# Reciprocal roots through Ln and Exp, and a final norm in three token parts, in a hybrid SSD and attention step on one core

## The chip, the cores and the metric

The kernel runs on one core of a Trainium2 chip. A core has five engines with a queue each: TensorE (PE in the profile, with its weight loads as PEld), VectorE (DVE), ScalarE (ACT), GpSimd (POOL, unused here) and SyncE (SP), which issues most DMA transfers. Each engine works through its own instructions in order and waits on semaphores for the others. The metric is the device time of one execution in microseconds (us).

## What is computed

One inference step of two layers over 640 tokens (512 latent, 128 prompt) and 1024 features: a Mamba-2 style SSD mixer in layer 0, differential attention in layer 1, a convolutional feed-forward block after each, and a final norm. Each sub-layer starts from a root mean square norm, and this norm is what the change rewrites:

```
def _rms(x):
    xf = x.astype(F32)
    return xf * lax.rsqrt(jnp.mean(xf * xf, axis=-1, keepdims=True) + EPS)

def rmsnorm(x, g):
    return (_rms(x) * g.astype(F32)).astype(x.dtype)

def modulate(x, g, shift, scale):
    return rmsnorm(x, g) * (1 + scale) + shift

def conv_ffn(h, up_w, conv_w, conv_b, down_w):
    u = dwconv(h @ up_w, conv_w, conv_b)
    a, v = jnp.split(u, 2, axis=-1)
    return (jax.nn.silu(a) * v) @ down_w

for i in range(DEPTH):
    x = x + gate_mix * mixer[i % 2](modulate(x, norm_mix_g, shift, scale))
    x = x + gate_ffn * conv_ffn(modulate(x, norm_ffn_g, shift, scale))
y = rmsnorm(x, final_norm_g)
```

The loop is a shortened form of the reference's own. In the SSD mixer the output is also normed in four feature groups, and in attention each of the eight heads' outputs is normed over its 128 features; all of these take a reciprocal root per token.

## The kernel before

**Layout.** Activations are feature-major: `x` is eight tiles of 128 features by 640 tokens. Tokens fall in two "halves", A = columns 0 to 255 and B = columns 256 to 639, the last 128 of which are the prompt. Every dense product is done in three passes, with weights and activations each split in a rounded high part and the rest (`whi`, `wlo` and `h..h`, `h..l`): high by high, high by low, low by high. A weight tile arrives by DMA in `raw`, ScalarE copies it to `whi` (line 131) and VectorE subtracts to get `wlo` (line 132).

**Order of the work.** The class `Step` emits dense products as the main stream. Other work is written as generators in a queue of tasks: after each feature tile of a product a hook (line 71) advances every task that is due, and a generator's `yield n` says in how many hooks it wants to go on. A scheduler of the language then orders each engine's instructions, so that an engine's own order can differ from the order of the code; the groups of VectorE operations in a root are interleaved with other work in the trace.

**PSUM.** Dense products and attention scores share a pool of three two-bank tiles (tag `d`). Sums `ms`, transposes and broadcasts use one bank with tag `m` or one with tag `y`.

**The root.** `rms_bcast` (line 173) sums squares over features with a matrix of ones on TensorE (`ms`, four groups of a quarter of the tokens), calls `rsqrt` (line 161), yields, and then spreads the result to all partitions with a selecting matrix (`nbc` for the norms of `x`, `obc` for a head, `gbc` for an SSD group). `rsqrt` works on 128 by n values, n a quarter of the tokens: 64 for A, 96 for B, 160 for all tokens. It is a scale and shift (`rs_v`, line 166), an integer seed (line 167) and three Newton steps of three VectorE operations each (lines 169 to 171), eleven in all. It is called 21 times: once at the start, four times in the SSD mixer (`ssd_norm`), for both halves of the three norms between sub-layers (`norm_task`), for the eight heads (`att_tail`) and for both halves of the final norm (`final_task`).

**The end of a sub-layer.** `project_last` (line 259) makes the eight output tiles. The first five are done one after the other for both halves. The last three are done half by half: first A for each of the three tiles, then B, tile 5 alone and tiles 6 and 7 together. After a tile's product `gate_add` (line 247) adds it to `x` on VectorE and `norm_sq` squares it on ScalarE. Behind a half's last tile the next norm for this half is queued with a delay of three hooks.

**The final norm.** `final_task` (line 1001) forms, per half, eight output tiles `yt` on VectorE, in temporary buffers that rotate over four, each followed by its DMA issue on SyncE. At the end of the program the queued tasks are run to their ends in order (line 1069).

**Attention.** Per head, `att_head` makes a score product `sl` into a `d` tile for each of four query blocks and two maps, VectorE takes row maxima (`sm`), ScalarE the exponentials `e` with their sums, and `att_tail` transposes the weights (`wt`), multiplies them with the values (`ov`), takes the squares (`osq`) and the head's root. This runs between the products of the next head's q, k and v tiles.

**Activation tables.** [...] The kernel before uses Tanh, Exp, Silu, Square, Copy and Identity.

## Time and profile before

| What | us |
|---|---|
| Runs of the kernel, median of 3 (lowest, highest) | 1979.58 (1979.57, 1981.41) |
| Profiled execution, first to last instruction (span) | 1977.5 |
| TensorE busy in it | 1905.5 |
| VectorE busy | 1418.0 |
| ScalarE busy | 905.2 |

The profiled execution's own device time is not recorded beside its span; the median of the runs lies 2.1 us above the span. In the views below, a row of the timeline has the start, the duration, the engine, the line, the operation and what it writes and reads; in square brackets stands the idle time of the engine before it and what ended that. A row of the windows has the window and its length, then the busy time and number of instructions of PE, PEld, DVE, ACT and POOL, then the granted TensorE clock as a share of full speed, the DMA share and GB/s. A row of the groups has the count, the busy time and the mean of one in ns, then the idle time ahead.

### The profile page before, as it was taken

What the parts mean: (1) busy time and instruction counts of PE and PEld (TensorE: products, weight loads), DVE (VectorE), ACT (ScalarE), POOL (GpSimd) and SP (SyncE); (2) the same over time, 40 slices, a digit from 0 to 9 for tenths busy, and PEclk for the clock granted to TensorE, in tenths of its full rate; (3) what the DMA queues carried; (4) which work ended last, traced back from release to release, by engine and by line L of the source; (5) the groups of instructions that cost most, each with busy time, mean ns of one, the idle gap of its engine ahead of it and who ended that gap; (6) DMA issues with size and microseconds to landing.
All of it is one profiled execution on the core that took longest, in us unless ns stands there. A gap on an engine that the chain in (4) does not pass through costs nothing.

```text
span 1977.5 us, 33157 instructions
## 1 busy us (share of the span) xinstructions
PE 1905.5 (96%) x13453; PEld 1788.0 (90%) x13453; DVE 1418.0 (72%) x2745; ACT 905.2 (46%) x1702; POOL 0.2 (0%) x4
## 2 busy tenths in 40 slices
PE   6899999999999999999999989999999999999997
PEld 3678989888999999999999978988899999999997
DVE  4658899998977888688675788888868553553554
ACT  2337677676834432133133466666635331331331
POOL 0000000000000000000000000000000000000000
PEclk9999999999999999999999989999999999999999
DMA  8454212112232244444442221111022222222211
GB/s 303 153 191 143 75 44 81 49 65 79 91 98 68 96 149 141 144 142 142 144 136 70 70 69 38 49 49 38 21 93 75 75 75 75 77 67 83 73 57 54
DMA packets 62121, 184.98 MB, mean 94 GB/s; under 512 B 7824, under 2 KB 14224, under 8 KB 61840
## 3 DMA queue, kind: packets, MB, share of 16 engines
q1 hardware_dynamic: 61968, 182.86, 28.4%
q8 instruction: 106, 1.74, 0.4%
q14 instruction: 47, 0.39, 0.1%
HBM read 177.06 MB, written 5.77 MB: 92 GB/s over the span
## 4 chain that ended last, share of the span: by engine, by line
PE 76%; DMA 11%; DVE 7%; ACT 3%; issue 3%; SPq 0%; DVEq 0%; ACTq 0%
PE up L99 19%; PE po L99 18%; DMA mw<-in_modT 10%; PE z L99 6%; PE x L99 5%; PE st L99 5%; DVE junk L454 3%; PE bc L99 3%; PE yp L99 3%; PE q L99 3%; PE k L99 2%; PE v L99 2%; PE sl L99 2%; PE modrow L99 1%; PE ov L99 1%
## 5 line engine op out<-in xcount | busy, mean ns | idle before, releaser
L90 ACT ACTIVATE whi<-raw 128x1024 fp32r<-128x1024 f32 (+4 forms) x230 | 235.9, 1027 | 422.4 <-PE po L99 182.3
L96 DVE TENSOR_TENSOR wlo<-raw,whi 128x1024 fp32r<-128x1024 f32 (+4 forms) x230 | 270.2, 1177 | 164.2 <-ACT whi L90 162.8
L93 DVE SCALAR_TENSOR_TENSOR xr<-po,mod,xr 128x256 f32<-128x256 f32 (+1 forms) x231 | 89.7, 434 | 125.6 <-PE po L99 125.4
L454 DVE CUSTOM_DVE_ANT_0 junk<-mw,cbc 128x1024 f32<-128x1024 f32 x96 | 116.4, 1221 | 75.7 <-DMA mw<-in_modT 75.6
L99 PE MATMUL po<-mh,whi 128*128 128x256 f32 (+1 forms) x704 | 167.8, 310 | 0.8 <-DVE ca L93 0.8
L99 PE MATMUL po<-mh,wlo 128*128 128x256 f32 (+1 forms) x704 | 167.3, 310 | 0.0
L99 PE MATMUL po<-ml,whi 128*128 128x256 f32 (+1 forms) x704 | 167.2, 309 | 0.0
L99 PE MATMUL up<-h01h,whi 128*128 128x256 f32 (+1 forms) x656 | 151.3, 312 | 9.7 <-DVE ca L93 5.8
L99 PE MATMUL up<-h11h,whi 128*128 128x256 f32 (+1 forms) x656 | 149.4, 309 | 2.7 <-DVE ca L93 2.7
L99 PE MATMUL up<-h01l,whi 128*128 128x256 f32 (+1 forms) x656 | 150.4, 310 | 0.0
L99 PE MATMUL up<-h01h,wlo 128*128 128x256 f32 (+1 forms) x656 | 150.4, 310 | 0.0
L99 PE MATMUL up<-h11h,wlo 128*128 128x256 f32 (+1 forms) x656 | 149.4, 309 | 0.0
L99 PE MATMUL up<-h11l,whi 128*128 128x256 f32 (+1 forms) x656 | 149.4, 309 | 0.0
L99 PEld LDWEIGHTS up<-h01h,whi 128*128 128x128 f32 x656 | 119.8, 189 | 11.9 <-issue 8.1
L99 PEld LDWEIGHTS po<-mh,whi 128*128 128x128 f32 x704 | 128.3, 188 | 1.3 <-issue 1.0
L99 PEld LDWEIGHTS po<-mh,wlo 128*128 128x128 f32 x704 | 128.4, 188 | 0.0
L99 PEld LDWEIGHTS po<-ml,whi 128*128 128x128 f32 x704 | 128.2, 188 | 0.2 <-DVE ml L96 0.2
L99 PEld LDWEIGHTS up<-h11h,whi 128*128 128x128 f32 x656 | 119.3, 188 | 3.0 <-ACT whi L90 3.0
L99 PEld LDWEIGHTS up<-h01l,whi 128*128 128x128 f32 x656 | 120.4, 189 | 0.0
L99 PEld LDWEIGHTS up<-h01h,wlo 128*128 128x128 f32 x656 | 120.3, 189 | 0.0
L99 PEld LDWEIGHTS up<-h11h,wlo 128*128 128x128 f32 x656 | 119.3, 188 | 0.0
L99 PEld LDWEIGHTS up<-h11l,whi 128*128 128x128 f32 x656 | 119.3, 188 | 0.0
(489 smaller groups left out, 4451.3 us busy)
## 6 DMA issues: line engine op xcount, KB each, us to landing
raw<-in_w_up SPq DMA_DIRECT2D x88, 512.0 KB, 3.5
mw<-in_modT SPq DMA_DIRECT2D x48, 512.0 KB, 4.4
raw<-in_w_in SPq DMA_DIRECT2D x40, 512.0 KB, 3.6
mr<-in_mod SPq DMA_DIRECT2D x32, 512.0 KB, 4.0
raw<-in_w_dn SPq DMA_DIRECT2D x32, 448.0 KB, 3.3
raw<-in_w_qkv SPq DMA_DIRECT2D x24, 512.0 KB, 3.5
mp<-in_modp SPq DMA_DIRECT2D x32, 256.0 KB, 5.4
raw<-in_w_so SPq DMA_DIRECT2D x16, 512.0 KB, 3.6
```

Of the source, the lines that this page charges most:

```text
L90: return self.nc.scalar.activation(out, in_, func, **k)
L93: return self.nc.vector.scalar_tensor_tensor(out, in0, s, in1, op0, op1)
L96: return self.nc.vector.tensor_tensor(out, a, b, op)
L99: return self.nc.tensor.matmul(out, lhsT, rhs, start=start, stop=stop)
L454: nc.vector.tensor_tensor_reduce(j, w, cb[:, c, :], 1.0, 0.0, ALU.mult, ALU.add, self.mod[l][:, t, c:c + 1])
```

## The change

Every root but those of the SSD groups takes its first value from two ScalarE functions, exp(-0.5 ln(ms / count + eps)), and then makes one Newton step instead of three. The last `project_last` of the program (in the feed-forward block of layer 1) makes its last three tiles in three token parts, A (256 columns), M (256, the rest of the latent tokens) and Q (128, the prompt). Its last group differs too: M and Q do the three tiles one by one, and only a part named B does tiles 6 and 7 together. The final norm has these three parts. A and M write each output tile to a buffer of the large pool and issue its DMA on SyncE; M waits 99 hooks after its broadcast, which leaves its outputs to the end; Q writes all eight outputs into one tile and issues two DMAs of four tiles each, the first on SyncE and the second on ScalarE. The remaining tasks are run to their ends last first. Comments and docstrings go, which is all that most of the diff does; those parts are left out here.

```diff
-HALF = {"A": (A0, A1), "B": (A1, B1)}
+HALF = {"A": (A0, A1), "B": (A1, B1), "M": (A1, TS), "Q": (TS, B1)}
-COND = {"A": ((0, 256, 1),), "B": ((256, 512, 1), (512, 640, 0))}
+COND = {"A": ((0, 256, 1),), "B": ((256, 512, 1), (512, 640, 0)), "M": ((256, 512, 1),), "Q": ((512, 640, 0),)}
...
-    def rsqrt(self, y, ms, n, count):
+    def rsqrt(self, y, ms, n, count, power):
         V.tensor_scalar(v, ms, 1.0 / count, EPS, ALU.mult, ALU.add)
-        V.tensor_scalar(y.bitcast(I32), v.bitcast(I32), -0.5, RSQRT_MAGIC, ALU.mult, ALU.add)
-        for _ in range(3):
+        if power:
+            self.act(y, ms, AF.Ln, scale=1.0 / count, bias=self.eps)
+            self.act(y, y, AF.Exp, scale=-0.5)
+        else:
+            V.tensor_scalar(y.bitcast(I32), v.bitcast(I32), -0.5, RSQRT_MAGIC, ALU.mult, ALU.add)
+        for _ in range(1 if power else 3):
...
-    def rms_bcast(self, alloc, sq, t0, t1, count, wait=4):
+    def rms_bcast(self, alloc, sq, t0, t1, count, wait=4, power=True):
-        self.rsqrt(y, ms[:, :n], n, count)
+        self.rsqrt(y, ms[:, :n], n, count, power)
...
-        tag = {"A": "y", "B": "m"}[half]
+        tag = {"A": "y", "B": "m", "M": "y", "Q": "m"}[half]
...
-    def project_last(self, h, ks, g, nextnorm, ks_last=None):
+    def project_last(self, h, ks, g, nextnorm, ks_last=None, parts="AB"):
...
-        for hf, groups in (("A", (ws[0:1], ws[1:2], ws[2:3])), ("B", (ws[0:1], ws[1:3]))):
-            for grp in groups:
+        for hf in parts:
+            for grp in ((ws[0:1], ws[1:3]) if hf == "B" else (ws[0:1], ws[1:2], ws[2:3])):
...
+        self.eps = self.ct([P, 1], "eps")
+        nc.vector.memset(self.eps, EPS)
...
-                self.project_last(mid, range(k0, k1), self.gate(l, 1), nextnorm)
+                self.project_last(mid, range(k0, k1), self.gate(l, 1), nextnorm, parts="AMQ" if l else "AB")
...
-        bc = yield from self.rms_bcast(lambda: self.wide("gbc"), [sq], 0, T, 512)
+        bc = yield from self.rms_bcast(lambda: self.wide("gbc"), [sq], 0, T, 512, power=False)
...
-    def final_task(self, half):
-        bc = yield from self.norm_stats(half)
-        c0, c1 = HALF[half]
+    def final_task(self, part):
+        nc = self.nc
+        bc = yield from self.norm_stats(part)
+        c0, c1 = HALF[part]
+        if part == "M":
+            yield 99
+        gain = lambda i: self.gains[:, 4 * KT + i:4 * KT + i + 1]
+        if part == "Q":
+            n = c1 - c0
+            y = self.pw.tile([P, 1024], F32, tag="raw", name="yq", bufs=RAW)
+            for i in range(KT):
+                self.stt(y[:, i * n:(i + 1) * n], self.x[i][:, c0:c1], gain(i), bc[:, :n], ALU.mult, ALU.mult)
+                if i % 4 == 3:
+                    eng = nc.sync if i == 3 else nc.scalar
+                    eng.dma_start(self.a["yT"][i - 3:i + 1, :, c0:c1].rearrange("i p c -> p i c"),
+                                  y[:, (i - 3) * n:(i + 1) * n].rearrange("p (i c) -> p i c", i=4))
+            return
         for i in range(KT):
-            t = self.tmp("yt")
-            self.stt(t[:, c0:c1], self.x[i][:, c0:c1], self.gains[:, 4 * KT + i:4 * KT + i + 1], bc[:, :c1 - c0],
-                     ALU.mult, ALU.mult)
-            self.nc.sync.dma_start(self.a["yT"][i, :, c0:c1], t[:, c0:c1])
+            t = self.slot("f", f"yt{i}", bufs=NF)
+            self.stt(t[:, c0:c1], self.x[i][:, c0:c1], gain(i), bc[:, :c1 - c0], ALU.mult, ALU.mult)
+            nc.sync.dma_start(self.a["yT"][i, :, c0:c1], t[:, c0:c1])
             yield 1
...
-            for t in list(self.tasks):
+            for t in reversed(list(self.tasks)):
                 self.drain(t)
```

## The prediction

> **What bounds the kernel now.** I read the page's totals first, then busy time by stage, then the chain of waits at the end.

> ```profile
> span 1977.5 us, 33157 instructions
> PE 1905.5 (96%) x13453; PEld 1788.0 (90%) x13453; DVE 1418.0 (72%) x2745; ACT 905.2 (46%) x1702; POOL 0.2 (0%) x4
> L90 ACT ACT_TABLE_LOAD x4 | 5.1, 1283 | 2.9 <-DVE sg L816 1.7 <-PEq L1160 0.7 <-DVE ca L93 0.5
> 1120.00:1480.00 360.00, 342.30 (x2237) 315.38 (x2237) 292.14 (x606) 225.65 (x455) 0.00 (x0) 0.98 0.15 49
> ```

> TensorE (PE, the first pair in a window's row) is busy 96% of the span, so an edit counts only where it starts or stops TensorE waiting, or shortens the end, where TensorE has run dry. The third row counts ScalarE's activation-table loads: four in the whole program, 1.28 us each. In attention (1120 to 1480) TensorE is idle only 18 us of 360, ScalarE (the fourth pair) is busy 226.

> **The change part by part.**

> *Table loads.* Of the 21 reciprocal roots, the four group norms of the SSD mixer keep the old form. The other 17 and one more (the final norm now has three parts) become 18 with Ln and Exp. In the changed program's ScalarE order every one of these 18 has a table load ahead of its Ln and another ahead of its Exp: 39 loads where there were 4 (with the first one, and two ahead of Silu; the old load ahead of the attention's first Exp is gone). ScalarE therefore gets 35 x 1.28 = 45 us of loads.

> [...]

> *DVE's relief.* A root loses the integer seed and two of three Newton steps, seven VectorE operations, and gains two ScalarE ones.

> ```profile
> 1964.51 0.27 DVE rs_v L166
> 1967.39 0.27 DVE rs_y L93
> 1967.80 2.01 PE nbc L99 x8
> L90 ACT ACTIVATE m<-r,Ctok 128x128 f32<-128x128 f32 x160 | 61.9, 387 | 0.0
> ```

> Uncontended, the old chain (eleven VectorE operations, the first and the last shown) runs from 1964.51 to 1967.66: 3.15 us, 0.29 each. The new one is the scale (0.27), Ln, a load (1.28), Exp and three VectorE operations (0.85). Ln and Exp are not in the trace; the nearest row, a ScalarE op with a bias operand on 128x128, has 0.39, and I take 0.3 (between 0.2, the smallest ops here, and 0.4). Sum 3.0 us when ScalarE idles long enough to hide the load ahead of Ln, up to 4.3 when not. The chain gains nothing, and ScalarE is blocked for 2 x 1.28 + 0.3 = 2.9 us up to the end of the second load. Seven VectorE operations saved per root lie in stages where TensorE does not wait for them: worth 0 to 0.5 us each time, I take 0.

> *Attention, eight roots.* Heads 1 to 5 repeat every 37.3 us; of head 4's norm:

> ```profile
> 1335.09 0.80 ACT L90 ACTIVATE e<-sl,sm 128x640 f32<-128x640 f32 x1
> 1335.86 0.80 ACT L90 ACTIVATE e<-sl,sm 128x640 f32<-128x640 f32 x1
> 1336.56 0.20 ACT L90 ACTIVATION_READ_ACCUMULATOR e<-sl,sm 128x1 f32 x1
> 1336.04 0.56 PE L99 MATMUL q<-h10h,whi 128*128 128x256 f32 x2 [1.07 <-ACT e L90]
> 1337.02 0.46 PE L99 MATMUL sl<-kh,qs 128*128 128x320 f32 x2
> ```

> The softmax exponentials `e` free the three rotating PSUM tiles; TensorE already waits 1.07 us for the first. The order listing puts load, Ln, load exactly between these two exponentials. The second then ends at 1336.76 + 2.9 = 1339.7, and the score product of 1337.02, which takes its PSUM tile, stands at the head of TensorE's queue until then, with the rest of the q tile behind it: 2.65 us each, 13.3 for five.

> ```profile
> 1199.23 0.28 ACT L90 ACTIVATE wpT<-wpt 128x128 f32<-128x128 f32 x1 [0.40 <-PE wpt L934]
> 1199.92 0.60 PE L951 MATMUL wt<-cst,w 128*128 128x128 f32 x4
> 1411.25 0.80 ACT L90 ACTIVATE e<-sl,sm 128x640 f32<-128x640 f32 x1 [0.84 <-DVE sm L890]
> 1412.33 0.46 PE L99 MATMUL sl<-kh,qs 128*128 128x320 f32 x2
> ```

> Head 0's loads stand ahead of the weight cast and the copy `wpT` that frees the bank for the transposes of 1199.92: the copy ends near 1203.5, 3.6 us of wait. Head 6 has 0.84 us of ScalarE idle to absorb: 2.35 late at 1411.25, 2.2 at 1412.33. Head 7's root falls in an idle ScalarE: 0. Together 19.1 us; lower bound 10 (half hidden by rescheduled gaps), upper 24 (no gap absorbs).

> *Clock.* Such waits also cost TensorE its clock:

> ```profile
> 654.20 0.87 PE L99 MATMUL up<-h01h,whi 128*128 128x256 f32 x2 [3.52 <-ACT whi L90]
> 654.20:657.00 2.80, 2.80 (x10) 2.80 (x11) 2.74 (x7) 1.99 (x2) 0.00 (x0) 0.50 0.00 0
> 840.51 0.53 PE L99 MATMUL up<-h01h,whi 128*128 128x256 f32 x2 [2.28 <-DVE ca L93]
> 841.50:845.00 3.50, 3.50 (x15) 3.50 (x15) 2.25 (x3) 2.36 (x3) 0.00 (x0) 0.54 0.40 138
> 1515.46 0.54 PE L99 MATMUL up<-h11h,whi 128*128 128x256 f32 x2 [2.75 <-DVE ca L93]
> 1515.50:1518.50 3.00, 3.00 (x21) 3.00 (x22) 2.94 (x8) 2.10 (x3) 0.00 (x0) 1.00 0.02 5
> ```

> The granted clock (third figure from the end) is 0.50 for about 3 us after 3.52 us of idle and 0.54 after 2.28, but 1.00 after 2.75. A drop costs half of 3 us, 1.5. [...] I count half of seven long waits (six here, one below): 5.3 us, bounds 0 and 10.

> *Norms between layers, six roots.* These have sums `ms`, then other products, then the broadcast `nbc`, at places the scheduler moved.

> ```profile
> 1115.43 0.37 PE L99 MATMUL ms<-sq,cst 128*32 128x96 f32 x8
> 1115.98 0.25 DVE L166 TENSOR_SCALAR rs_v<-ms 128x96 f32<-128x96 f32 x1
> 1119.82 1.10 PE L99 MATMUL nbc<-rs_y,cst 128*128 128x96 f32 x8
> 1476.32 0.54 PE L99 MATMUL ms<-sq,cst 128*32 128x64 f32 x24
> 1478.31 0.33 PE L99 MATMUL po<-o5h,wlo 128*128 128x384 f32 x1
> 1479.78 1.10 PE L99 MATMUL nbc<-rs_y,cst 128*128 128x64 f32 x8
> ```

> At 1115.98 the order listing has 22 products of 256 columns (2.6 us) between them where there were 31: the broadcast is reached at 1118.4, while two loads, a small Exp and the Ln and copies between bring the root to 1121.0: 2.6 us of wait. At 1476.86 it has 10 products of 384 (1.75 us) for 16: reached at 1478.6, ready at 1480.2, 1.6 us. The other four: 0.5 twice, 0.6 where the modulation's Tanh stands between the loads, 0 once. Sum 5.8; bounds 1 (later gaps give it back) and 9. The very first root may come 1 us earlier or later and is hidden, since the following stage waits for weights.

> *The last three tiles and the end.* Token half B (384 columns) becomes M (256) and Q (128).

> ```profile
> 1949.12 0.28 PE L99 MATMUL po<-ml,whi 128*128 128x256 f32 x1
> 1949.23 0.28 PE L99 MATMUL po<-mh,wlo 128*128 128x256 f32 x1
> 1949.53 0.33 PE L99 MATMUL po<-ml,whi 128*128 128x384 f32 x1
> 1949.70 0.34 PE L99 MATMUL po<-mh,wlo 128*128 128x384 f32 x1
> 1969.83 0.62 DVE yt L93
> 1974.05 0.61 DVE yt L93
> ```

> Products start 0.117 us apart at 256 columns and 0.173 at 384, each with a weight load; the line through both gives 0.06 at 128, and 0.117 is the ceiling; I take 0.07. So 63 x 0.173 = 10.9 us becomes 63 x (0.117 + 0.07) = 11.8. M starts at 1949.35 and ends, with A's sums (0.6), broadcast (0.9) and a 0.4 wait, at 1958.65. Behind it VectorE still writes A's eight outputs until 1958.8, ahead of M's last two additions, so M's sums wait 1.0 us into Q; nine Q products later M's broadcast stands on TensorE's queue and waits 2.7 us for its root. Q ends near 1968.2, its squares at 1969.45, its root with both loads (none hidden: 1.28 twice, Ln, Exp, 0.75, pauses) at 1973.5, its broadcast at 1974.9, eight outputs of 0.26 at 1977.0. The last output ends today at 1974.05 + 0.61 and the span 2.84 us later; so the end goes to 1979.8, with some half clock in Q: +3.0. Bounds: -2.6 (Q's loads free) and +7 (0.117 and half clock). Sixteen output issues of SyncE come earlier than Q's and delay nothing.

> Sum: 19.1 + 5.3 + 5.8 + 3.0 = 33.2; 1977.5 becomes 2010.7. The runs' median, 1979.58, is 2.1 above the profiled span, so 2012.8; I say **2012**.

> **Rivals.**

> *Dearer loads.* ScalarE might have to empty itself ahead of each load.

> ```profile
> 651.90 2.00 ACT L90 ACTIVATE whi<-raw 128x1024 fp32r<-128x1024 f32 x2
> 654.17 1.28 ACT L90 ACT_TABLE_LOAD   x1 [0.27 <-DVE ca L93]
> 655.47 0.74 ACT L90 ACTIVATE ca<-ca 128x640 f32<-128x640 f32 x1
> ```

> Here 0.27 us lie ahead of the load, for which VectorE answers, and 0.02 behind it, which speaks against; but no load of before follows at once on a busy ScalarE. At one more load's length a load, the six attention waits grow by 2.6 each and norms and end by about 6: 2012 + 22 = 2034. [...] Chance 0.13.

> *Loads hidden.* ScalarE is free 134 us of attention's 360; if waits are made up before the next head, only the end and a few norms remain: +3 +4, 1986. The 18 us of TensorE idle there speak against: there is nothing to make them up from. Chance 0.11.

> *Faster: VectorE's relief decides.*

> ```profile
> 1330.00:1341.00 11.00, 9.93 (x70) 8.86 (x69) 9.22 (x26) 8.34 (x20) 0.00 (x0) 1.00 0.10 36
> 1341.00:1367.40 26.40, 26.40 (x173) 24.62 (x172) 22.11 (x39) 16.67 (x33) 0.00 (x0) 1.00 0.12 38
> ```

> In one head's period VectorE (third pair) works 31.3 us and ScalarE 25.0. If the exponentials come late because VectorE hands them their row maxima late, seven operations of 0.25 less per head (1.75) remove the 1.07 us wait of heads 1 to 5 and some 3 us of head 6's, -8; with the end at +3 and the norms even, 1979.6 - 5 = 1974.6. It decides once ScalarE has 2.9 us free ahead of the second exponential, so that both loads run there. For: ScalarE has 2.7 of the first 11 us free. Against: none of it lies between 1335.09 and 1336.76, where the loads stand, and TensorE's own work already fills 36.3 of 37.4 us. Chance 0.04; no change at all (the gains and one or two waits cancel), 0.02.

> **How the numbers follow.** Forecast 0.70. Within its own terms the bounds add to 8 and 50, seldom all at once: 1994 to 2030, which leaves out most of the dearer loads and of the hidden ones, about 2 in 10. A measurement of this kernel tells 0.2% (4 us) from no change. Slower by more: forecast, dear loads and hidden loads, 0.94; within 0.02; faster 0.04.

> **What would show it.** Right: 39 table loads of 1.28 us; TensorE waiting about 2.7 us for ScalarE's `e` once a head at a score product, head period near 40 to 41.5 us; waits at `nbc` near the old 1118 and 1479; a wait of over 2 us at `nbc` inside Q. Wrong: head period still near 37.3; a load without its own row; products of 128 columns over 0.117 us apart; ScalarE order other than listed.

## The result and the profile after

| | us | ratio to before, 95% interval |
|---|---|---|
| Before, median of 4 runs on this chip | 1980.49 | |
| Changed, median of 4 runs | 2022.79 (2021.14 to 2026.27) | 1.0216 [1.0202, 1.0231] |
| Predicted | 2012 (1994 to 2030) | |

The kernel became slower by 42.3 us, where I had said 32. The execution profiled below took 2026.27 us, the longest of the four, so its span is 46.6 us above the earlier one. The first lines are from the page of the changed kernel: its span, its busy time and its group of table loads.

```profile
span 2024.1 us, 33313 instructions
PE 1937.9 (96%) x13556; PEld 1816.1 (90%) x13556; DVE 1395.4 (69%) x2639; ACT 962.1 (48%) x1776; POOL 0.2 (0%) x4
L90 ACT ACT_TABLE_LOAD x39 | 50.0, 1283 | 1.6 <-PEq L1181 0.7 <-DVE ca L93 0.3
```

There are 39 loads of 1283 ns instead of 4 (ACT_TABLE_LOAD, a row of its own on ScalarE): 18 stand directly ahead of a root's Ln and 18 between this Ln and the root's Exp. VectorE lost 22.6 us of work and TensorE is busy 32.4 us longer, though it has only 103 matmuls more.

**Attention.** From the root of head 0 to that of head 7, these windows of the kernel before (first) and of the changed one show where the time went:

```profile
1198.40:1447.60 249.20, 240.42 (x1577) 221.13 (x1578) 204.94 (x416) 161.04 (x325) 0.00 (x0) 0.99 0.12 39
```

```profile
1202.70:1481.40 278.70, 254.28 (x1577) 232.52 (x1578) 196.81 (x366) 183.98 (x354) 0.00 (x0) 0.94 0.11 35
```

The same 1577 products take 29.5 us longer. Length less PE's busy time is TensorE's idle time: 8.8 before, 24.4 now, so 15.6 us are new waits. The other 13.9 us are the products themselves, at a granted clock of 0.94 instead of 0.99. One head of the changed kernel shows both. The timeline of ScalarE, where the root's loads fall, comes first, then that of TensorE:

```profile
1312.72 0.81 ACT L90 ACTIVATE e<-sl,sm 128x640 f32<-128x640 f32 x1
1313.39 0.22 ACT L90 ACTIVATION_READ_ACCUMULATOR e<-sl,sm 128x1 f32 x1
1313.63 1.28 ACT L90 ACT_TABLE_LOAD   x1
1314.92 0.39 ACT L90 ACTIVATE rs_y<-ms,eps 128x160 f32<-128x160 f32 x1
1315.34 1.28 ACT L90 ACT_TABLE_LOAD   x1
1316.63 0.79 ACT L90 ACTIVATE e<-sl,sm 128x640 f32<-128x640 f32 x1
...
1317.42 0.32 ACT L90 ACTIVATE rs_y<-rs_y 128x160 f32<-128x160 f32 x1
```

```profile
1313.66 0.56 PE L99 MATMUL q<-h10h,whi 128*128 128x256 f32 x2 [1.07 <-ACT e L90]
...
1317.57 0.85 PE L99 MATMUL sl<-kh,qs 128*128 128x320 f32 x2 [2.46 <-ACT e L90]
```

The two loads and the Ln hold ScalarE from 1313.63 to 1316.62, exactly between two exponentials `e`. No idle time is shown ahead of either load, so it costs its 1.28 us and nothing more, on a ScalarE that was busy until then. TensorE's wait of 1.07 us was there before; the 2.46 is new, and five heads have it within 0.02 us. The windows right behind it:

```profile
1313.70:1317.60 3.90, 1.44 (x9) 1.18 (x9) 1.12 (x3) 3.86 (x6) 0.00 (x0) 1.00 0.41 134
1317.60:1320.00 2.40, 2.40 (x9) 2.40 (x10) 1.66 (x5) 1.01 (x3) 0.00 (x0) 0.51 0.00 0
1320.00:1323.00 3.00, 3.00 (x20) 2.96 (x19) 1.63 (x5) 2.05 (x4) 0.00 (x0) 0.82 0.02 5
1323.00:1326.00 3.00, 3.00 (x21) 2.74 (x20) 3.00 (x5) 1.87 (x5) 0.00 (x0) 1.00 0.00 0
```

The clock is 0.51 for 2.4 us and 0.82 for 3.0: 2.4 x 0.49 + 3.0 x 0.18 = 1.7 us of full-clock time lost. (The trace has one stretch at 0.50 there, from 1317.66 to 1321.07; the windows cut it.) With the 2.46 that is the new head period, 41.6 us for 37.4.

**Norms between layers.** TensorE's rows for their broadcasts:

```profile
639.86 1.10 PE L99 MATMUL nbc<-rs_y,cst 128*128 128x96 f32 x8 [1.50 <-DVE rs_y L93]
...
1122.65 1.59 PE L99 MATMUL nbc<-rs_y,cst 128*128 128x96 f32 x8 [1.77 <-DVE rs_y L93]
...
1514.08 1.10 PE L99 MATMUL nbc<-rs_y,cst 128*128 128x64 f32 x8 [1.42 <-DVE rs_y L93]
...
1533.15 1.10 PE L99 MATMUL nbc<-rs_y,cst 128*128 128x96 f32 x8 [0.56 <-DVE rs_y L93]
```

Their four waits are 5.25 us together; a fifth broadcast waits 0.35 us, where it had waited for nothing.

**The end.** From the root of A's final norm to the end of the span the changed kernel takes 36.6 us, the kernel before 25.7. TensorE's timeline there, behind M's sums:

```profile
1997.56 0.27 PE L99 MATMUL po<-ml,whi 128*128 128x128 f32 x1
1997.67 0.28 PE L99 MATMUL po<-mh,wlo 128*128 128x128 f32 x1
2000.52 1.94 PE L99 MATMUL nbc<-rs_y,cst 128*128 128x64 f32 x8 [2.57 <-DVE rs_y L93]
2002.21 0.45 PE L99 MATMUL po<-mh,whi 128*128 128x128 f32 x1
...
2011.42 0.41 PE L99 MATMUL po<-ml,whi 128*128 128x128 f32 x1
2011.64 0.41 PE L99 MATMUL po<-mh,wlo 128*128 128x128 f32 x1
...
2016.74 1.46 PE L99 MATMUL nbc<-rs_y,cst 128*128 128x32 f32 x6 [3.57 <-DVE rs_y L93]
```

```profile
2002.20:2005.00 2.80, 2.80 (x15) 2.80 (x15) 2.51 (x7) 0.31 (x1) 0.00 (x0) 0.50 0.31 105
2005.00:2008.00 3.00, 3.00 (x16) 3.00 (x16) 1.32 (x4) 0.01 (x1) 0.00 (x0) 0.50 0.75 252
2008.00:2012.00 4.00, 4.00 (x22) 3.88 (x22) 0.00 (x0) 0.30 (x1) 0.00 (x0) 0.50 0.00 0
```

Q's products of 128 columns start 0.112 us apart ahead of the wait (1997.56 and 1997.67) and 0.213 behind it (2011.42 and 2011.64, the mean of 45 of them). TensorE is busy without a gap from 2002.2 to 2012, and the clock stays at 0.50 all the time.

### The profile page after: what moved, and what is told of

Its sections match the earlier page's. It is cut to its first block, busy times and chain, and to the rows that moved or that the text cites. A ratio compares the mean times of both kernels' runs of the same rounds, so it can differ in the third digit from the quotient of the medians.

```text
span 2024.1 us, 33313 instructions
## 1 busy us (share of the span) xinstructions
PE 1937.9 (96%) x13556; PEld 1816.1 (90%) x13556; DVE 1395.4 (69%) x2639; ACT 962.1 (48%) x1776; POOL 0.2 (0%) x4
## 4 chain that ended last, share of the span: by engine, by line
PE 79%; DMA 8%; ACT 6%; DVE 5%; issue 2%; SPq 0%; DVEq 0%; ACTq 0%
PE up L99 21%; PE po L99 20%; DMA mw<-in_modT 6%; PE z L99 6%; PE x L99 5%; PE st L99 3%; PE bc L99 3%; PE yp L99 3%; PE k L99 2%; PE q L99 2%; PE v L99 2%; DVE junk L462 2%; ACT L90 2%; PE sl L99 2%; PE modrow L99 1%
## 5 line engine op out<-in xcount | busy, mean ns | idle before, releaser
L90 ACT ACTIVATE whi<-raw 128x1024 fp32r<-128x1024 f32 (+4 forms) x230 | 235.9, 1027 | 422.3 <-PE po L99 176.1
L93 DVE SCALAR_TENSOR_TENSOR xr<-po,mod,xr 128x256 f32<-128x256 f32 (+1 forms) x231 | 89.6, 434 | 135.1 <-PE po L99 134.8
L99 PE MATMUL po<-mh,whi 128*128 128x256 f32 (+2 forms) x725 | 174.5, 310 | 0.6 <-DVE ca L93 0.6
L99 PE MATMUL po<-ml,whi 128*128 128x256 f32 (+2 forms) x725 | 173.9, 310 | 0.0
L99 PE MATMUL po<-mh,wlo 128*128 128x256 f32 (+2 forms) x725 | 173.9, 310 | 0.0
L99 PE MATMUL up<-h01h,whi 128*128 128x256 f32 (+1 forms) x656 | 151.1, 311 | 5.2 <-ACT whi L90 3.5
L99 PE MATMUL up<-h11h,whi 128*128 128x256 f32 (+1 forms) x656 | 149.4, 309 | 1.5 <-DVE ca L93 1.5
L99 PE MATMUL up<-h01l,whi 128*128 128x256 f32 (+1 forms) x656 | 150.3, 310 | 0.0
L99 PE MATMUL up<-h01h,wlo 128*128 128x256 f32 (+1 forms) x656 | 150.3, 310 | 0.0
L99 PE MATMUL up<-h11h,wlo 128*128 128x256 f32 (+1 forms) x656 | 149.4, 309 | 0.0
L99 PE MATMUL up<-h11l,whi 128*128 128x256 f32 (+1 forms) x656 | 149.4, 309 | 0.0
L99 PEld LDWEIGHTS po<-mh,whi 128*128 128x128 f32 x725 | 134.5, 191 | 1.2 <-issue 0.8
L99 PEld LDWEIGHTS po<-mh,wlo 128*128 128x128 f32 x725 | 134.6, 191 | 0.0
L99 PEld LDWEIGHTS po<-ml,whi 128*128 128x128 f32 x725 | 134.4, 191 | 0.2 <-DVE ml L96 0.2
L99 PEld LDWEIGHTS up<-h01h,whi 128*128 128x128 f32 x656 | 119.8, 189 | 7.1 <-ACT whi L90 3.8
L99 PEld LDWEIGHTS up<-h11h,whi 128*128 128x128 f32 x656 | 119.2, 188 | 1.8 <-ACT whi L90 1.8
L99 PEld LDWEIGHTS up<-h01l,whi 128*128 128x128 f32 x656 | 120.4, 189 | 0.0
L99 PEld LDWEIGHTS up<-h01h,wlo 128*128 128x128 f32 x656 | 120.2, 189 | 0.0
L99 PEld LDWEIGHTS up<-h11h,wlo 128*128 128x128 f32 x656 | 119.3, 188 | 0.0
L99 PEld LDWEIGHTS up<-h11l,whi 128*128 128x128 f32 x656 | 119.2, 188 | 0.0
```

Source lines behind the costliest of these rows:

```text
L90: return self.nc.scalar.activation(out, in_, func, **k)
L93: return self.nc.vector.scalar_tensor_tensor(out, in0, s, in1, op0, op1)
L99: return self.nc.tensor.matmul(out, lhsT, rhs, start=start, stop=stop)
```

## The experiments

The runs below were made beside runs of the kernel before on the same chip (experiments 1 to 4 on one, the others on a second), which had medians of 1978.7 to 1979.0 us there and single runs between 1971.8 and 1984.6; each ratio is to those. This table, from the profiled executions (the first two columns are the profiles shown above), cuts each span at the first VectorE operation `rs_v` of a root (us):

| From root to root | before | changed | changed again | old root | loads only | old end | one set | first root old |
|---|---|---|---|---|---|---|---|---|
| start to the first SSD root | 243.7 | 246.7 | 246.3 | 243.1 | 247.5 | 249.2 | 247.2 | 243.4 |
| to norm A ahead of feed-forward 0 | 369.4 | 369.3 | 369.3 | 369.4 | 369.4 | 369.4 | 369.4 | 369.4 |
| to norm A ahead of attention | 488.1 | 485.6 | 489.0 | 485.5 | 483.8 | 485.7 | 487.2 | 490.7 |
| to the root of head 0 | 97.2 | 101.1 | 97.8 | 95.9 | 99.7 | 101.0 | 93.7 | 93.4 |
| to the root of head 7 | 249.2 | 278.7 | 275.0 | 249.5 | 273.9 | 276.1 | 248.8 | 248.6 |
| to norm A ahead of feed-forward 1 | 29.4 | 29.4 | 29.4 | 29.4 | 29.4 | 29.4 | 29.4 | 29.4 |
| to the final norm's A | 474.8 | 476.7 | 476.8 | 474.3 | 474.7 | 476.0 | 472.7 | 473.4 |
| to the end | 25.7 | 36.6 | 36.6 | 32.4 | 25.6 | 26.4 | 27.4 | 23.3 |

The third row varies by some us with no order in it; no cause is read from it.

### 1. The old root, the new end

```diff
-    def rms_bcast(self, alloc, sq, t0, t1, count, wait=4, power=True):
+    def rms_bcast(self, alloc, sq, t0, t1, count, wait=4, power=False):
```

> The changed kernel with the integer seed and three Newton steps in all 19 roots; the last three output tiles and the final norm stay in three token parts. Theory (two table loads a root cost the attention and the norms, and the three parts cost the end by themselves, because products of 128 columns start 0.112 us apart at full clock and 0.213 us apart at the half clock that follows the wait of the broadcast): 4 table loads, head period back at 37.3 us, and only the end is dearer than before, by 5 to 9 us: 1986 to 1990 us. Rival one (all of the loss comes from the loads, Q's slow clock included): 1978 to 1982 us. Rival two (a good part of the loss in the attention does not come from the roots): above 2000 us.

Measured: 1983.77 us, ratio 1.0029 [1.0015, 1.0043]: 5.1 us above the kernel before, the foot of the 5 to 9 expected (the times in the text were reckoned from 1980.5). The attention is back at 249.5 us, the end is 32.4. So the end in three parts costs by itself, and nothing in the attention is left without the new root. A shorter wait is enough for the end's clock. M's broadcast waits 1.52 us here, and the products behind it run at 0.112 us apart for a further 1.1 us; then:

```profile
1960.00:1961.50 1.50, 1.50 (x14) 1.50 (x14) 1.20 (x4) 0.00 (x0) 0.00 (x0) 0.85 0.00 0
1961.50:1963.00 1.50, 1.50 (x9) 1.50 (x9) 1.50 (x5) 0.00 (x0) 0.00 (x0) 0.50 0.75 253
1963.00:1968.30 5.30, 5.30 (x26) 5.19 (x25) 0.87 (x3) 0.31 (x1) 0.00 (x0) 0.50 0.38 126
```

### 2. The new root, the old end

```diff
-                self.project_last(mid, range(k0, k1), self.gate(l, 1), nextnorm, parts="AMQ" if l else "AB")
+                self.project_last(mid, range(k0, k1), self.gate(l, 1), nextnorm)
...
-            for t in reversed(list(self.tasks)):
+            for t in list(self.tasks):
```

(The final task is that of the kernel before.)

> The changed kernel with the last three output tiles and the final norm in two token parts, as before; the roots keep Ln, Exp and one Newton step (37 table loads, for 17 roots). Theory: the attention and the norms stay as dear as in the changed kernel (about +36 us where the last part begins), and the end gives back 5 to 9 us of its 10.8, for the last root still has both loads on its path: 2013 to 2018 us. Rival (the three parts are as cheap as the prediction's +3 had them, since they shorten the last part): 2019 to 2024 us.

Measured: 2015.32 us, 1.0188 [1.0173, 1.0203]. The end takes 26.4 us, 0.7 more than before: with two parts, the two loads on the last root's way cost little. The new root alone costs 36.6 us; with the 5.1 us of the first experiment that is 41.7 of the 42.3.

### 3. The same way over ScalarE without loads

```diff
-            self.act(y, ms, AF.Ln, scale=1.0 / count, bias=self.eps)
-            self.act(y, y, AF.Exp, scale=-0.5)
+            self.act(y, ms, AF.Identity, scale=1.0 / count, bias=self.eps)
+            self.act(y, y, AF.Copy, scale=0.001)
```

> The changed kernel with Identity in the place of Ln and Copy in the place of Exp, so that each root still goes through ScalarE twice but needs no table: 4 loads. The roots' values are other than the reference's. Theory (the loads' 1.28 us each make the waits; ScalarE's two operations alone cost 0.25 us each): the waits of 2.46 us at the score products shrink to 0.6 us or nothing, the head period to 37.3 to 38 us, and the time to 1986 to 1993 us, the rest being the end. Rival (the way over ScalarE as such, or its order, makes the waits): head period above 40 us and 2010 us or more.

Measured: 1976.56 us, 0.9980 [0.9965, 0.9996]; the waits of 2.46 us are gone and the head period is 37.6 us. It came out 9 us below the range I had set. I had added the dear end to the old time (its end takes 30.3 us, 4.6 more than before) and left out that without loads two stages ahead of it gain: 92.6 us for 97.2 to the root of head 0, and 472.7 for 474.8 to the final norm's A. The experiments with one table set show both again. Its third stage is also 4.4 us shorter and its first 4.4 longer.

### 4. The old kernel with loads that nobody needs

```diff
+        if power:
+            m = min(n, 96)
+            w = self.pc.tile([P, 96], F32, tag="rs_w", name="rs_w", bufs=1)[:, :m]
+            self.act(w, v[:, :m], AF.Ln)
+            self.act(w, w, AF.Exp)
```

> The kernel before, with its own root and its own end, and beside each of 17 roots one Ln and one Exp on ScalarE into a scratch tile that nothing reads: 37 table loads at the places where the changed kernel has them. This is added work. Theory (what counts is that ScalarE is held for 2.8 us between two exponentials, whoever reads the result): the attention loses what it loses in the changed kernel, head period 41 to 42 us, and the time is 2008 to 2018 us. Rival (the loads cost only where the root itself waits for them, and VectorE's chain now runs beside them): 1980 to 1990 us.

Measured: 2008.76 us, 1.0157 [1.0136, 1.0178]. The attention takes 273.9 us, TensorE's wait at the score product is 2.52 us, and the head period 41.4. The root's result came 3.5 us later after its `rs_v` than before (11.9 for 8.4 us), but nothing waited for it: its broadcast followed at 15.9 us without idle time on TensorE. ScalarE being held is enough. It makes 30.1 of the 36.6 us of the second experiment.

### 5. The changed kernel again

> The changed kernel once more, beside the next three on one chip. In its first profile the end took 36.6 us from the last A root to the end of the span, where the kernel before takes 25.8, and the 45 last products of Q started 0.213 us apart. Theory (that follows from the program and not from that execution): again 34 to 37 us, again 0.213 us for at least 25 of these products; head roots 41.6 us apart; 2018 to 2025 us. Rival (the end of that profile was an accident, for the time of its run was 4 us above the median of the others): an end of 28 to 32 us.

Measured: 2022.46 us, 1.0228 [1.0209, 1.0247]; the end again 36.6 us, 45 products of Q again 0.213 us apart. The slow end belongs to the program. In the attention the waits are the same and the slow products cost 9.9 us instead of 13.9.

### 6. M's broadcast behind all of Q

```diff
-        return self.rms_bcast(lambda: self.bank(tag, "nbc"), self.nsq, *HALF[half], D, 3)
+        return self.rms_bcast(lambda: self.bank(tag, "nbc"), self.nsq, *HALF[half], D, 99 if half == "M" else 3)
...
-        if part == "M":
-            yield 99
...
-            for t in reversed(list(self.tasks)):
+            for t in list(self.tasks):
```

> The changed kernel with M's broadcast behind all products of Q, so that TensorE has no wait between the sums of M and the last product; nothing else moves. Theory A (the products of 128 columns lower the clock by themselves, since TensorE is loading weights for half of their time: without TensorE's long wait, in the runs with the old root and without table loads, the clock fell to 0.50 some 2 us into them): the first 10 to 25 of the products behind M's sums 0.112 us apart and the rest 0.213. Theory B (the wait of 2.6 us lowers the clock, and the stream only fails to raise it): all of them 0.112 us apart. By A the end shortens by 2 to 5 us against the changed kernel, by B by 6 to 9; M's eight outputs come later in both and may give back 1 to 3 us.

Measured: the windows of Q's products, with no wait ahead of them, are

```profile
1996.70:2000.00 3.30, 3.30 (x38) 3.26 (x30) 0.55 (x3) 2.87 (x4) 0.00 (x0) 1.00 0.26 89
2000.00:2002.80 2.80, 2.80 (x27) 2.80 (x27) 0.96 (x4) 0.62 (x2) 0.00 (x0) 1.00 0.00 0
```

All 54 products behind M's sums start 0.112 us apart. Theory B holds here: without the wait the 128-column products kept the clock of 1.00 that they had. Theory A has TensorE loading weights for half of their time, which no run shows: the rows of the weight loads fill 3.26 of 3.30 us and all of 2.80 here. The end of this profile is 29.8 us, 6.8 less than the changed kernel's, although the last broadcast now waits 5.66 us for a root that stands behind M's outputs on VectorE. The timed gain is smaller, 2020.40 against 2022.46 us, 1.0216 [1.0198, 1.0235] beside 1.0228, and these intervals overlap; how much of the 6.8 us the other runs kept is open.

### 7. One table set for both functions

```diff
+        self.switch = count == D and t0 == 0
...
+            self.sq_last = self.act(self.nsq[i - KT + 4][:, c0:c1], x, AF.Square).ins
...
+            if self.switch:
+                pre = self.nc.scalar.preload_act_table_set("natural_log_exp_and_others")
+                order = mybir.DependencyInfo(mybir.DependencyClass.NoSync, mybir.DependencyReason.DATA)
+                self.tc.add_manual_dep(pre.ins, self.sq_last.name, order, reason="after the squares")
+                with self.tc.issue_after(pre.ins):
+                    self.act(y, ms, AF.Ln, scale=1.0 / count, bias=self.eps)
```

> The changed kernel with a single table set that holds both functions, loaded ahead of the Ln of the first root and of the A half of each norm, and kept from there (the set also serves the copies, squares and exponentials of the attention): 11 loads where there were 39, none of them in the eight heads; roots by Ln, Exp and one Newton step as changed. Theory (the loads are the whole cost of the new root): head roots 37.3 to 37.8 us apart, no wait above 0.3 us at the score products behind a root, and the time that of the changed kernel with the old root (0 to 6 us above the kernel before), for the end in three parts stays. Rival (Ln and Exp between two exponentials cost as such): heads above 39 us, 1995 us or more.

Measured: 1978.56 us, 1.0004 [0.9991, 1.0016]. The groups of table loads, 12 in all, those asked for by name in the second row:

```profile
L90 ACT ACT_TABLE_LOAD x7 | 9.0, 1283 | 4.0 <-DVE cacc L93 2.9 <-PEq L1189 0.7 <-DVE ca L93 0.3
L170 ACT ACT_TABLE_LOAD x5 | 6.4, 1283 | 0.1
```

ScalarE's timeline at the place shown above for the changed kernel:

```profile
1297.18 0.81 ACT L90 ACTIVATE e<-sl,sm 128x640 f32<-128x640 f32 x1
1297.86 0.22 ACT L90 ACTIVATION_READ_ACCUMULATOR e<-sl,sm 128x1 f32 x1
1297.95 0.41 ACT L90 ACTIVATE rs_y<-ms,eps 128x160 f32<-128x160 f32 x1
1298.23 0.82 ACT L90 ACTIVATE e<-sl,sm 128x640 f32<-128x640 f32 x1
```

The Ln stands between the same two exponentials, which now start 1.05 us apart instead of 3.91, and the score product behind them waits for nothing. In the heads it was the loads alone. The end is 27.4 us: M's broadcast waits 0.70 us, and this time all products behind it stay 0.112 us apart.

### 8. One table set and the old end

The edit of experiment 7 on the kernel of experiment 2.

> The same single table set, and the last three output tiles and the final norm in two token parts as in the kernel before: 11 loads. Theory (with the loads and the 128-column products gone, what is left of the change is its gain: seven VectorE operations fewer in 17 roots, 1.5 to 2 us off the last root, some tenths a head): 2 to 9 us under the kernel before, the end 23.5 to 25 us from the last A root instead of 25.8. Rival (the relief of VectorE is hidden everywhere, as I predicted of it): within 2 us of the kernel before.

Measured: 1976.73 us, 0.9990 [0.9979, 1.0000], 2.0 below, just at the edge of no change; the end 23.3 us. The attention gains no more than 0.5 us by VectorE's relief (248.7 us), but the last root does gain. At the start of attention the first score product waits 1.23 us where it had waited 3.0. It does so in all four kernels with one Newton step and no load in the heads (experiments 3, 7, 8 and 10), and it waits 3.0 us with the old root and with the loads; by which step was not tested.

### 9. M and Q exchanged in size

```diff
-HALF = {"A": (A0, A1), "B": (A1, B1), "M": (A1, TS), "Q": (TS, B1)}
+HALF = {"A": (A0, A1), "B": (A1, B1), "M": (A1, 384), "Q": (384, B1)}
```

(`COND` goes with it, and Q's outputs are written as A's are.)

> The changed kernel with the sizes of the two last parts exchanged: M has the 128 columns (tokens 256 to 383) and Q 256 (384 to 639); all three parts write their outputs as A does. All 39 loads stay. By the experiment with the late broadcast the wait behind M's sums puts the clock at 0.50, and 128-column products never got it back in 9.8 us. Theory (the width decides whether the clock comes back: 256 columns keep TensorE's array busy enough): M's products 0.112 us apart at full clock; behind the wait of its broadcast Q's products start at 0.21 to 0.24 us and are back at 0.117 within 2 to 4 us, so that Q's 54 products take 7 to 8.5 us. Rival (what counts is only that the wait falls so near the end, and no stream recovers there): 0.23 us apart to the last, 11 to 13 us. Time, by theory, 2016 to 2023 us: Q is dearer at its root and outputs, cheaper by the clock.

Measured: 2029.83 us, 1.0256 [1.0240, 1.0272], so my time was wrong. That the clock comes back was right, a little later than I had said. A's broadcast now stands in the 128-column stream and waits 1.75 us; M's products behind it are 0.213 us apart from 1992.4 on. TensorE's timeline where Q begins and where its clock changes (M's sums stand between), then the windows around it:

```profile
1997.73 0.41 PE L99 MATMUL po<-mh,wlo 128*128 128x128 f32 x1
1997.94 0.52 PE L99 MATMUL po<-mh,whi 128*128 128x256 f32 x1
...
2002.35 0.38 PE L99 MATMUL po<-ml,whi 128*128 128x256 f32 x1
2002.56 0.29 PE L99 MATMUL po<-mh,wlo 128*128 128x256 f32 x1
2002.69 0.28 PE L99 MATMUL po<-mh,whi 128*128 128x256 f32 x1
```

```profile
1994.00:2000.00 6.00, 6.00 (x29) 5.87 (x28) 0.84 (x3) 1.73 (x3) 0.00 (x0) 0.50 0.31 104
2000.60:2002.40 1.80, 1.80 (x20) 1.74 (x12) 0.19 (x1) 1.33 (x2) 0.00 (x0) 0.50 0.00 0
2002.40:2003.30 0.90, 0.90 (x7) 0.71 (x6) 0.36 (x2) 0.47 (x2) 0.00 (x0) 0.91 0.00 0
```

128 columns left the clock at 0.50 for 5.6 us, from 1992.3 to 1997.9. Behind them came products of 256 columns, as far apart (0.213 us), nine ahead of M's sums and eight behind, and the clock was back 4.6 us after the first of them; I had expected 2 to 4. Apart from the sums, only the columns per product differ. TensorE is busy without a gap in both windows (6.00 of 6.00 us, 1.80 of 1.80), so its busy time does not show the reason that the theory gives. The end takes 40.6 us, 4.0 more than in the changed kernel. Q, the last part, now has twice the columns left for its root and its outputs: from the start of its last product to the end of the span it takes 17.7 us for 12.5. The 4.0 us are about half of the 7.4 between the two kernels' times; the rest lies ahead of the end.

### 10. The first root old as well

```diff
-        st = self.rms_bcast(lambda: self.wide("nbc"), self.nsq, 0, T, D)
+        st = self.rms_bcast(lambda: self.wide("nbc"), self.nsq, 0, T, D, power=False)
```

> The kernel of the last experiment (single table set, two token parts at the end) with one more edit: the very first root, before the SSD mixer, has its integer seed and three Newton steps again. In every kernel whose first root goes over ScalarE the second root comes 2.6 to 4.4 us later than in the kernel before (246.3 to 248.1 us against 243.7), with and without table loads there, and in the one with the old root everywhere 0.6 us earlier. Theory (the first root's way over ScalarE makes this, by the order of the products behind it or a load ahead of the first Tanh): the second root at 243 to 244.5 us, and the run 2 to 4 us under the kernel of the last experiment, 0.2 to 0.4 per cent under the kernel before. Rival (the start varies by itself, or later waits take it back): no change against the last experiment's 0.999.

Measured: 1973.54 us, 0.9969 [0.9956, 0.9982]. The second root comes at 243.4 us instead of 247.6. This version is faster than both kernels, 0.3% faster than the kernel before: Ln and Exp from one set in 16 roots, the end in two token parts, the old form in the first root. The last broadcast of the kernel before, then that of this one:

```profile
1967.80 1.99 PE L99 MATMUL nbc<-rs_y,cst 128*128 128x96 f32 x8 [3.36 <-DVE rs_y L93]
```

```profile
1962.74 1.10 PE L99 MATMUL nbc<-rs_y,cst 128*128 128x96 f32 x8 [2.04 <-DVE rs_y L93]
```

It waits 2.04 us where the kernel before waited 3.36.

## Why the prediction was right, and where its terms were off

The direction, the main mechanism (loads between two exponentials, and TensorE waiting at the score product behind them) and the order of size were right; the time lay in the range, 11 us above the value. That it stayed there was in part luck: the end came out above its own bound of 7, the clock in attention at 13.9 and 9.9 us about its bound of 10, and the first root had been put at nothing, while the waits in attention came out below their value. Term by term, from the profiles:

| Term | predicted | measured | what showed it |
|---|---|---|---|
| waits in attention | 19.1 | 15.6 | windows, experiments 3, 4, 7 |
| clock behind them | 4.5 of 5.3 | 13.9, again 9.9 | windows of one head |
| waits of the norms | 5.8 | 5.3 | `nbc` rows |
| the end | 3.0 | 10.9 | experiments 1, 2, 6, 9 |
| first root | hidden | 3.0 | experiment 10 |

The measured terms make 48.7 us. The two spans differ by 46.6: the stage up to norm A ahead of attention was 2.5 us shorter in this profile (third row of the table of stages, which varies without a known cause).

**Table loads.** 39 of 1283 ns, in the order listed. "Dearer loads" falls: 37 of the 39 start 0.02 us behind the row ahead of them on ScalarE, the other two 0.72 us (the first of the program) and 0.27 us.

**Waits in attention.** The place and the cause were right for heads 1 to 5 (2.46 each for 2.65) and head 6 (2.28 for 2.2). Head 0 was over-priced: 1.9 us in two waits for 3.6. The changed program loaded a table ahead of each Ln and again ahead of each Exp (39 loads); with one set asked for by name (experiment 7, 12 loads) there was no load in the heads at all.

**Clock.** This term failed by its count. "A drop costs half of 3 us, 1.5" was near (1.7 in the head shown), but I counted half of the waits; in the head shown, with 1.07 and 2.46 us of wait within 4 us, the clock fell, and the head period is the same 41.6 us in at least three of heads 1 to 5 of either profile, so it fell in each. The rest up to 13.9 lies in the other heads and in second stretches at half clock, and 4 us of it came and went between two profiles of one kernel.

**Norms.** The sum held, two of its parts did not: 1.50 for 0.6 where the Tanh stands between the loads, 1.77 for 2.6 at the broadcast of 1122.65. That these two misses nearly cancel is luck.

**The end.** The step that failed is "the line through both gives 0.06 at 128, and 0.117 is the ceiling; I take 0.07". The ceiling was the value: 0.112 at full clock. And behind M's wait, which came as predicted (2.57 for 2.7), the clock fell and stayed, which the "some half clock in Q" had at 0.7 us. Eighteen products at 0.112 and 45 at 0.213 are 11.6 us where I had 63 x 0.07 = 4.4, and the broadcast at half clock took 1.94 for 0.9: 8.2 us, and 7.5 of them beyond the 0.7, nearly all of the 7.9 missed. A row of the prediction itself showed this clock: the eight products of the last broadcast of the kernel before took 2.01 us (1.99 in the timeline), where those of two others took 1.10. Q's root (3.57 us of wait) and its outputs took about what I had. Products of 128 columns over 0.117 us apart were one of the signs that I had named for being wrong.

**The first root.** "Is hidden, since the following stage waits for weights" was wrong: wherever it went over ScalarE, the next root came 2.6 us or more later, and experiment 10 undid it. In experiment 4, where the old root only has Ln and Exp beside it, the next one is 3.9 us later too, with 20 products of `modrow` ahead of its broadcast, so their number does not decide it. In the changed kernel no load lies behind it; its broadcast stands behind 16 products of `modrow` where it stood behind 20, and TensorE's order behind it differs too. By which step the time goes is open.

**Rivals.** "Loads hidden" falls with experiments 3 and 4. "VectorE's relief decides" has its mechanism wrong: the 1.07 us wait stays in experiment 7, with seven VectorE operations fewer. The relief shows elsewhere once the loads are gone: experiment 10 is 5.4 us below the kernel before.

## What to carry to other kernels

The table loads hurt here by where they stood, not by what waited for their functions (30.1 of 36.6 us in experiment 4, where nothing read the results): look for what else is queued on ScalarE behind a load, and for one set that serves the whole stage (12 loads for 39 in experiment 7, and 1978.56 us for 2022.46). When products are cut into narrower ones, price them at the pace of wider ones until a trace shows less (0.112 us at 128 columns for 0.117 at 256 here), and put no wait ahead of a narrow stream at the end (0.213 us apart behind a wait of 2.57 us, 0.112 with none). Keeping the last part wide was worth some 7 us here (ratio 1.0188 for 1.0216 and 1.0228); moving the wait behind the narrow stream shortened the end of one profile by 6.8 us, of which the times show 2, not clear of noise.

## What the runs showed of the hardware that was not expected

```profile
1954.89:1958.30 3.41, 2.71 (x25) 2.66 (x24) 2.08 (x8) 0.31 (x1) 0.00 (x0) 1.00 0.04 15
1958.30:1961.71 3.41, 3.41 (x19) 3.41 (x17) 2.31 (x7) 0.31 (x1) 0.00 (x0) 0.50 0.77 259
```

```profile
1957.10:1960.51 3.41, 2.71 (x51) 2.49 (x50) 0.90 (x4) 0.68 (x3) 0.00 (x0) 1.00 0.24 82
1960.51:1963.92 3.41, 3.41 (x33) 3.41 (x32) 3.18 (x9) 0.31 (x1) 0.00 (x0) 1.00 0.42 143
```

TensorE is busy 2.71 us in both stretches with the wait, so neither the length of the wait nor the busy time tells the two apart. The products that start there have 2560 columns in experiment 3, and 3840 in experiment 7, where M's sums fall into the same stretch.
